# Start and end of a two-layer decoder trunk: load order, an input block shared between engines, and the last squares and a product moved to VectorE and GpSimd

## The chip, the core and the metric

The kernel runs on one core of a Trainium2 chip. The metric is the device time of one execution in microseconds (us); the kernel before takes 969.67 us (median of 3 runs, 969.65 to 970.43). Engines are named as in the profile: PE (TensorE; PEld is its weight load), DVE (VectorE), ACT (ScalarE), POOL (GpSimd), SP (SyncE, which issues most transfers). ACT has a transfer queue of its own, written ACTq beside SPq.

## What is computed

Sixteen learned meta rows are put before 512 rows of x, and two layers follow: gated linear attention, then differential softmax attention. Each begins with an RMS norm and ends in a residual add. A last RMS norm drops the meta rows. Both stretches that the change touches are norms:

```python
def rmsnorm(x, g):
    xf = x.astype(jnp.float32)
    y = xf * lax.rsqrt(jnp.mean(xf * xf, axis=-1, keepdims=True) + EPS)
    return (y * g.astype(jnp.float32)).astype(x.dtype)

h = jnp.concatenate([meta, x], axis=1)      # 16 + 512 rows of 1024
for i in range(DEPTH):
    hn = rmsnorm(h, g_norm[i])
    ...
return rmsnorm(h[:, N_META:], g_final)
```

## The kernel before, in words

Work on the 528 rows is float32; products are split into a high and a low part, so each matrix product is three passes on PE. Weights stream in by SP and are split by ACT (high part) and DVE (low part). PE's order is written out by hand over the whole program; ACT's and DVE's orders are written out by hand at the start (from `squares(0)` on), and DVE's again in the last call `F0(1)`. Elsewhere a scheduler orders them, so a change of the program's text can move rows there too.

**The start.** The rows come in five blocks: block 0 is the 16 meta rows, blocks 1 to 4 are 128 rows of x each, `xt[0]` to `xt[4]` (in the profile: tiles `z`, `qs`, `ks`, `v`, `v`). SP issues, in order: `ident` (identity matrix, 64 KB), meta (64 KB), x blocks 1 and 2 (512 KB each), `grows` (both norms' gains, 8 KB, tile `vm`), x blocks 3 and 4, `glr_raw` (tile `a`, 16 columns of weights in pieces of 64 bytes), then weights `raw`. For each block

- `squares(b)` (L712) lets ACT square the block's 1024 columns and sum them per row,
- `factor(b)` (L564, L565) turns the sum into a row factor: one small op on DVE, then a power on POOL,
- `scaled(b)` (L722) lets DVE multiply the block by its factor, in two halves of 512 columns,
- `raw_turn` (L730) and `turned` (L742) transpose on PE the raw rows and the first half of the scaled rows,
- `raw_copy` (L736, L738) moves the raw transposes to SBUF.

PE transposes only the first half of each block there; the second halves follow for all blocks at once. When block 4's first half is transposed, `scaled_pair` (L800 on ACT, L801 on DVE) multiplies by the gain `g_sb`, and from there the first projections follow. `g_sb` (L775) and `xm`, the meta columns times the gain (L777, tile `t`), are made on DVE after `factor(4)`; `glr` (L779 on ACT, L780 on DVE, tile `kd`) is the split of `glr_raw`. PE runs filler products `warm_up` (L656) between these steps.

**The end.** `final_rows(b, ...)` adds the last products to row block b (`hacc`, tile `keep`, L1857), squares and sums it (L1858 on ACT), makes the row factor (tile `fst`) and multiplies by it and by the gain `gfin`. Block 0 is last and is cut in columns 0 to 512, 512 to 768 and 768 to 1024:

```python
def finish(i, cs):
    hc = hacc[:, b, cs]
    dve.tensor_tensor(hc, hc, ps[i], op=ALU.add)
    act.activation(o[:, cs], hc, AF.Square, scale=..., accum_out=st[:, i:i + 1])
```

After the three sums DVE adds them (L1870, L1871), makes `hg`, the first half times the gain (L1872), POOL takes the power (L1873), ACT scales `hg` (L1882), DVE makes the second half (L1880), and each half goes out by a transfer of its own (L1883; ACT's queue for the first, SP's for the second).

Of the kernel before, what the change touches and what calls it, by code (L numbers as in the profile page):

```python
# [11 lines left out]
F32 = mybir.dt.float32  # L12
# [3 lines left out]
AF = mybir.ActivationFunctionType  # L16
ALU = mybir.AluOpType
# [10 lines left out]
KT = D // P  # L28
# [3 lines left out]
RANK = 16  # L32
EPS = 1e-6
# [184 lines left out]
def trunk(ctx, tc, x, meta, g_norm, gla_w_in, gla_w_gate_up, gla_b_gate, gla_gnorm, gla_w_out,  # L218
# [365 lines left out]
    gp = gctx.enter_context(tc.tile_pool(name="gp", bufs=1))  # L584
# [62 lines left out]
    mhalf = cp.tile([P, 8], F32, name="mhalf")  # L647
# [5 lines left out]
    def warm_up(n, t=None):  # L653
        t = warm if t is None else t
        for _ in range(n):
            pe.matmul(t[:, :P], ones, ones, start=True, stop=True)  # L656
# [2 lines left out]


    ident = cp.tile([P, P], F32, name="ident")
    sp.dma_start(ident, c_ident)
    xt = []
    grows = T(gp, [16, P], F32, "vm0")
    z2 = T(gp, [P, 2, D], F32, "z")
    v2 = [T(gp, [P, 2, D], F32, f"v{i}") for i in range(2)]
    for b in range(5):
        t0, n = BLK[b]
        t = T(gp, [P, D], F32, ("qs", "ks")[b - 1]) if b in (1, 2) else {0: z2, 3: v2[0], 4: v2[1]}[b][:, 1, :]
        sp.dma_start(t[:n], meta if b == 0 else x[(b - 1) * P:b * P])  # L670
        xt.append(t)
        if b == 2:
            sp.dma_start(grows, g_norm.rearrange("l (k p) -> (l k) p", p=P))
    glr_raw = T(gp, [P, KT, RANK], F32, "a0")
    sp.dma_start(glr_raw, g_w_in[:, 6144:6160].rearrange("(k p) c -> p k c", p=P))

# [21 lines left out]
    glr = T(gp, [P, KT, 112], F32R, "kd")  # L698
# [4 lines left out]

    yt = [T(gp, [P, 4, L], F32, f"y{i}") for i in range(2)]
    xm0 = v2[0][:, 0, :]
    sums0 = T(gp, [P, 10], F32, "sums0")
    raws = {}

    def squares(b):
        sq = z2[:, 0, :]  # L710
        n = BLK[b][1]
        act.activation(sq[:n], xt[b][:n], AF.Square, accum_out=sums0[:n, b:b + 1])  # L712

    def factor(b):
        n = BLK[b][1]
        rstd_of(sums0[:n, 5 + b:6 + b], sums0[:n, b:b + 1], D, n)

    def scaled(b, halves=range(2)):
        n = BLK[b][1]
        for i in halves:  # L720
            o = yt[i][:, b - 1, :512] if b else xm0[:NM, i * 512:(i + 1) * 512]
            dve.tensor_scalar(o, xt[b][:n, i * 512:(i + 1) * 512], sums0[:n, 5 + b:6 + b], None, op0=ALU.mult)  # L722

    def raw_turn(b, halves=range(2)):
        n = BLK[b][1]
# [6 lines left out]
    def raw_copy(b, i, eng):  # L732
        t0, n = BLK[b]
        o, pt = hT[:, 4 * i:4 * i + 4, t0:t0 + n], raws[b][i][:, :, :n]
        if eng is act:
            act.activation(o, pt, AF.Copy)  # L736
        else:
            dve.tensor_copy(o, pt)  # L738

    def turned(b, ks):  # L740
        for k in ks:
            pe.transpose(pts[k][:, (b - 1) * P:b * P], yt[k // 4][:, b - 1, k % 4 * P:(k % 4 + 1) * P], ident)  # L742
# [9 lines left out]
    pm0 = ps_tile()  # L752
    pm = pm0[:, :KT * NM].rearrange("p (k m) -> p k m", k=KT)
    for k in range(KT):
        pe.transpose(pm[:, k, :], xm0[:NM, k * P:(k + 1) * P], ident[:NM, :NM])
    raw_copy(1, 0, dve)
    squares(2)
    scaled(1)
# [5 lines left out]
    squares(3)  # L764
    scaled(2)
    factor(3)
    pe.transpose(pm0[:, KT * NM:KT * NM + 16], grows, ident[:16, :16])
    turned(2, range(4))
    warm_up(3)
    scaled(3)  # L770
    turned(3, range(4))
    squares(4)
    factor(4)
    g_sb = cp.tile([P, 2, KT], F32, name="g_sb")
    dve.tensor_copy(g_sb, pm0[:, KT * NM:KT * NM + 16].rearrange("p (l k) -> p l k", l=2))  # L775
    xm = tmp()[:, :KT * NM].rearrange("p (k m) -> p k m", k=KT)
    dve.tensor_tensor(xm, pm, g_sb[:, 0, :].unsqueeze(2).to_broadcast([P, KT, NM]), op=ALU.mult)  # L777
    for c in (0, 32, 64):
        act.activation(glr[:, :, c:c + RANK], glr_raw, AF.Copy)  # L779
    dve.tensor_tensor(glr[:, :, 96:], glr_raw, glr[:, :, :RANK].bitcast(F32), op=ALU.subtract)  # L780
    raw_copy(2, 0, act)
    raw_copy(2, 1, act)
    warm_up(3)
    scaled(4)
    turned(4, range(4))

    b12 = x_parts(6)
# [253 lines left out]
    halves = [(pg, slice(i * HT, (i + 1) * HT)) for i, pg in enumerate(pgs)]  # L1041
# [373 lines left out]
    hacc = T(kp, [P, 4, D], F32, "keep")  # L1415
# [98 lines left out]
    for m in range(2):  # L1514
# [4 lines left out]
        for i in range(2):  # L1519
            cs = slice(i * HT, (i + 1) * HT)  # L1520
# [323 lines left out]
    def final_rows(b, wt, yp):  # L1844

        cut = (0, 512, D) if b else (0, 512, 768, D)
        parts = [slice(c, e) for c, e in zip(cut, cut[1:])]
        ps = [(ps_tile() if i else pb_tile("bx"))[:, :cs.stop - cs.start] for i, cs in enumerate(parts)]
        o = T(xp, [P, D], F32, ("x1", "x3", "x2", "x1")[b], bufs=1)
        st = T(ep, [P, 8], F32, "fst")  # L1850
        hg = T(ep, [P, 512], F32, "t", bufs=3) if b == 0 else None
        if b:
            dve.memset(st[:, 2:3], 0.0)

        def finish(i, cs):
            hc = hacc[:, b, cs]
            dve.tensor_tensor(hc, hc, ps[i], op=ALU.add)  # L1857
            act.activation(o[:, cs], hc, AF.Square, scale=1.0 if b else float(D) ** -0.5, accum_out=st[:, i:i + 1])  # L1858

        def part(hd):  # L1860
            for i, cs in enumerate(parts):
                for n, (p, q, k) in enumerate([(0, q, k) for k in range(2) for q in range(2)] + [(1, 0, 0), (1, 0, 1)]):
                    pe.matmul(ps[i], yp[hd][p][:, k, b * P:(b + 1) * P],  # L1863
                              wt[q][cs.start // 512][:, 2 * hd + k, cs.start % 512:(cs.stop - 1) % 512 + 1],
                              start=hd == n == 0, stop=hd == 1 and n == 5)
                if hd:
                    finish(i, cs)
            if hd:
                if b == 0:
                    dve.scalar_tensor_tensor(st[:, 3:4], st[:, 0:1], EPS, st[:, 1:2], op0=ALU.add, op1=ALU.add)  # L1870
                    dve.tensor_tensor(st[:, 4:5], st[:, 2:3], st[:, 3:4], op=ALU.add)  # L1871
                    dve.tensor_tensor(hg, hacc[:, b, :512], gfin[:, :512], op=ALU.mult)  # L1872
                    pool.tensor_tensor(st[:, 4:5], st[:, 4:5], mhalf[:, :1], op=ALU.pow)  # L1873
                else:
                    dve.tensor_reduce(st[:, 3:4], st[:, 0:3], axis=AX.X, op=ALU.add)
                    rstd_of(st[:, 4:5], st[:, 3:4], D)
                for i in range(2):
                    cs = slice(512 * i, 512 * (i + 1))
                    if b or i:
                        dve.scalar_tensor_tensor(o[:, cs], hacc[:, b, cs], st[:, 4:5], gfin[:, cs], op0=ALU.mult, op1=ALU.mult)  # L1880
                    else:
                        act.activation(o[:, cs], hg, AF.Copy, scale=st[:, 4:5])  # L1882
                    (sp if b or i else act).dma_start(out[0, b * P:(b + 1) * P, cs], o[:, cs])  # L1883

        return part
# [19 lines left out]
    for hd in range(D_HEADS):  # L1905
# [13 lines left out]
        if not last:  # L1919
            n = heads[hd + 1]  # L1920
# [25 lines left out]
        for n, (f, b) in enumerate(steps):  # L1946
# [9 lines left out]
            if last and n == 5:  # L1956
                gfin = T(xp, [P, D], F32, "x0", bufs=1)
# [68 lines left out]
```

## Time and profile before

| what | value |
|---|---|
| median of 3 runs | 969.67 us |
| the profiled execution's own time | 971.08 us |
| its span in the profile | 968.4 us |
| busy share of the span, PE / DVE / ACT / POOL | 98% / 82% / 66% / 8% |
| granted clock of PE over the span | 0.996 |

The profile shows one execution, 2.7 us of which lie around the span, and which took 1.4 us more than the median. PE's busy share includes filler products at the start and pipelined products whose ends are modelled. A row of the timeline gives the start, the duration of the group, the engine, the line and what it writes and reads; the bracket at its end says how long the engine had been idle before and what released it.

### The profile page before, as it was taken

The numbers are of one execution on the slowest core, as the hardware profiler recorded it, in microseconds if no ns is written. First come the engines' busy times: TensorE is split into PE (matmuls) and PEld (weight loads), VectorE is DVE, ScalarE is ACT, GpSimd is POOL, SyncE is SP. The second block draws the span as 40 slices with busy tenths as digits, with TensorE's granted clock in tenths as the row PEclk, the third lists the DMA queues.
The fourth block names the chain that finished last, engine by engine and source line by source line (L and its number), as shares of the span: only waits on it lengthen the run. The fifth ranks groups of instructions, "written<-read, shape, count | busy, mean of one in ns | idle before, by whom it ended". The sixth has DMA issues, their size and how long they took to land.

```text
span 968.4 us, 18488 instructions
## 1 busy us (share of the span) xinstructions
PE 953.0 (98%) x7173; PEld 912.4 (94%) x7173; DVE 798.2 (82%) x1557; ACT 635.6 (66%) x1313; POOL 81.3 (8%) x164
## 2 busy tenths in 40 slices
PE   9999999999999999999999999999999999999997
PEld 8999999999999999998899898999999999989986
DVE  7989886886878787667997887879879889888875
ACT  7776755477647567656757685576766766755673
POOL 1000000000000000000001121111101101110111
PEclk9999999999999999999999999999999999999999
DMA  8322223635462237134356515234252261533312
GB/s 197 88 79 61 86 72 126 142 109 119 123 164 89 87 112 162 47 107 152 99 133 152 127 56 142 83 123 113 87 149 87 80 159 44 145 91 98 110 44 87
DMA packets 128602, 104.96 MB, mean 108 GB/s; under 512 B 51181, under 2 KB 112909, under 8 KB 128512
## 3 DMA queue, kind: packets, MB, share of 16 engines
q1 hardware_dynamic: 123184, 93.80, 35.3%
q10 hardware_dynamic: 5328, 9.95, 2.8%
q8 instruction: 57, 0.93, 0.4%
q14 instruction: 33, 0.27, 0.1%
HBM read 83.64 MB, written 11.80 MB: 99 GB/s over the span
## 4 chain that ended last, share of the span: by engine, by line
PE 73%; DVE 8%; ACT 4%; DMA 3%; issue 2%; POOL 1%; SPq 0%; POOLq 0%; DVEq 0%; ACTq 0%
PE bx L440 17%; PE bv L440 10%; PE by L440 9%; PE ps L409 7%; PE bx L997 5%; PE bx L430 4%; PE bx L409 3%; DMA raw<-in_diff_w_in_dram 3%; PE bv L997 2%; PE by L997 2%; PE ps L1239 2%; PE bv L409 1%; PE by L409 1%; DVE wl L285 1%; PE ps L1863 1%
## 5 line engine op out<-in xcount | busy, mean ns | idle before, releaser
L285 DVE TENSOR_TENSOR wl<-raw,wh 128x1024 fp32r<-128x1024 f32 x93 | 113.5, 1221 | 20.5 <-ACT wh L284 20.0
L284 ACT ACTIVATE wh<-raw 128x1024 fp32r<-128x1024 f32 x93 | 97.9, 1053 | 45.2 <-PE by L997 23.2
L440 PE MATMUL bv<-x,wh 128*128 128x264 f32 (+1 forms) x736 | 108.9, 285 | 0.1
L440 PE MATMUL bx<-x,wh 128*128 128x264 f32 (+1 forms) x720 | 105.6, 285 | 0.4 <-ACT ps L1777 0.4
L440 PEld LDWEIGHTS bv<-x,wh 128*128 128x128 f32 x736 | 96.8, 188 | 0.9 <-DVE z L497 0.3
L440 PEld LDWEIGHTS bx<-x,wh 128*128 128x128 f32 x720 | 94.4, 188 | 1.1 <-ACT ps L1777 0.7
L285 DVE TENSOR_TENSOR wl<-sum,wh 128x1024 fp32r<-128x1024 f32 x46 | 56.2, 1221 | 11.6 <-ACT wh L284 11.2
L461 ACT ACTIVATE u<-bx 128x264 f32<-128x264 f32 (+1 forms) x128 | 48.4, 378 | 21.8 <-PE bx L440 18.9
L440 PE MATMUL bv<-x,wl 128*128 128x264 f32 (+1 forms) x368 | 62.2, 286 | 0.1
L1735 ACT ACTIVATE p<-p,st 128x528 f32<-128x528 f32 (+3 forms) x64 | 36.4, 569 | 38.7 <-DVE st L1733 38.5
L440 PE MATMUL bx<-x,wl 128*128 128x264 f32 (+1 forms) x360 | 59.2, 284 | 0.0
L284 ACT ACTIVATE wh<-sum 128x1024 fp32r<-128x1024 f32 x46 | 48.4, 1051 | 10.4 <-PE bv L440 6.3
L440 PE MATMUL by<-x,a12h 128*128 128x264 f32 (+1 forms) x360 | 52.6, 285 | 0.9 <-DVE t L495 0.9
L440 PE MATMUL bx<-x,a11h 128*128 128x264 f32 (+1 forms) x360 | 53.0, 285 | 0.0
L440 PEld LDWEIGHTS bv<-x,wl 128*128 128x128 f32 x368 | 51.4, 188 | 0.4 <-issue 0.3
L284 ACT ACTIVATE a11h<-raw 128x512 fp32r<-128x512 f32 x46 | 28.9, 627 | 33.3 <-DMA raw<-in_diff_w_in_dram 12.8
L440 PEld LDWEIGHTS bx<-x,wl 128*128 128x128 f32 x360 | 50.0, 188 | 0.6 <-DVE wl L285 0.4
L440 PEld LDWEIGHTS bx<-x,a11h 128*128 128x128 f32 x360 | 47.8, 189 | 0.6
L440 PEld LDWEIGHTS by<-x,a12h 128*128 128x128 f32 x360 | 46.9, 188 | 1.1 <-DVE t L495 1.1
L565 POOL TENSOR_TENSOR st<-st,mhalf 128x1 f32<-128x1 f32 (+1 forms) x20 | 12.1, 606 | 386.5 <-DVE st L564 386.5
L1738 POOL TENSOR_TENSOR st<-st,minus 128x1 f32<-128x1 f32 x32 | 21.1, 658 | 279.4 <-ACT p L1735 226.4
L440 PE MATMUL by<-x,a22h 128*128 128x264 f32 (+1 forms) x280 | 40.1, 284 | 0.0
(501 smaller groups left out, 2671.8 us busy)
## 6 DMA issues: line engine op xcount, KB each, us to landing
raw<-in_diff_w_in_dram SPq DMA_DIRECT2D x52, 512.0 KB, 5.0
raw<-in_gla_w_in_dram SPq DMA_DIRECT2D x48, 512.0 KB, 4.5
raw<-in_gla_w_out_dram SPq DMA_DIRECT2D x8, 1024.0 KB, 6.0
raw<-in_diff_w_out_dram SPq DMA_DIRECT2D x8, 1024.0 KB, 5.3
raw<-in_diff_w_in_dram SPq DMA_DIRECT2D x6, 1024.0 KB, 6.0
vd<-planes ACTq DMA_DIRECT2D x12, 268.0 KB, 4.3
vd<-keep ACTq DMA_DIRECT2D x12, 264.0 KB, 2.3
T<-bdr SPq DMA_DIRECT2D x8, 264.0 KB, 3.8
```

The lines of the kernel that those rows point to most:

```text
L284: act.activation(hi, src, AF.Copy)
L285: dve.tensor_tensor(lo, src, hi.bitcast(F32), op=ALU.subtract)
L409: pe.matmul(ps, l, r, start=first and n == 0, stop=last and n == 2, **kw)
L430: pe.matmul(bank, a[:, k, :], b[k] if n0 is None else b[k][:, n0 + i * nn:n0 + (i + 1) * nn], start=n == 0 and ks[0] == 0, stop=n == len(t ...
L440: pe.matmul(bank[:, :x[q].shape[2]], w[p][:, k * P:(k + 1) * P], x[q][:, k, :], start=first and i == 0, stop=i == len(PASSES) - 1, skip_gr ...
L461: W.moved = act.activation(t, self.bx[:, :self.n], AF.Copy, scale=self.sc)
L565: pool.tensor_tensor(dst, dst, mhalf[:np_, :dst.shape[1]], op=ALU.pow)
L997: pe.matmul(banks[i][:, :HT], h.t[p][:, k, mm * P:(mm + 1) * P], s.y[q][k][:, i * HT:(i + 1) * HT], start=n == 0, stop=n == len(PASSES) - 1)
L1239: pe.matmul(o, s.kd[:, i, kc], s.qs[:, i, t0:t0 + n], start=i == 0, stop=i == 1)
L1735: act.activation(p[:, :nk], p[:, :nk], AF.Exp, scale=-1.0, bias=st[:, m:m + 1], accum_out=st[:, 2 + m:3 + m])
L1738: pool.tensor_tensor(st[:, 5:6], st[:, 3:4], minus, op=ALU.pow)
L1863: pe.matmul(ps[i], yp[hd][p][:, k, b * P:(b + 1) * P], wt[q][cs.start // 512][:, 2 * hd + k, cs.start % 512:(cs.stop - 1) % 512 + 1], star ...
```

## The change

Four things, in the diff's order.

1. SP issues x blocks 1 to 4 first; `ident`, meta and `grows` are issued by ACT, ahead of its table load. 
2. `squares(4)` is divided: ACT takes columns 0 to 512, DVE columns 512 to 1024 with a multiply-and-sum. `scaled(4)`'s first half goes to ACT, and one of block 2's raw copies goes from ACT to DVE.
3. `grows` is transposed before block 1 is, and `g_sb` and `xm` are made ahead of block 3's scaling. The low part of `glr` moves behind the first `scaled_pair`, and one filler product in PE's order goes.
4. In block 0 of the last norm the squares of the last 256 columns go to DVE, which adds the earlier sums on the way; `hg` goes to POOL and starts as soon as the first 512 columns are summed; the second half is made and sent in two pieces of 256 columns, so that SP issues two transfers.

```diff
-    sp.dma_start(ident, c_ident)
...
-    for b in range(5):
...
-        sp.dma_start(t[:n], meta if b == 0 else x[(b - 1) * P:b * P])
...
+    act.dma_start(ident, c_ident)
+    act.dma_start(xt[0][:NM], meta)
+    act.dma_start(grows, g_norm.rearrange("l (k p) -> (l k) p", p=P))
+    for b in range(1, 5):
+        sp.dma_start(xt[b], x[(b - 1) * P:b * P])
...
+    def squares(b, e=D):
...
+        act.activation(sq[:n, :e], xt[b][:n, :e], AF.Square, accum_out=sums0[:n, b:b + 1])
+        if e < D:
+            dve.tensor_tensor_reduce(sq[:n, e:], xt[b][:n, e:], xt[b][:n, e:], op0=ALU.mult, op1=ALU.add, scale=1.0,
+                                     scalar=D * EPS, accum_out=sums0[:n, 10:11])
...
+            dve.tensor_scalar(o, sums0[:n, b:b + 1], sums0[:n, 10:11], 1.0 / D, op0=ALU.add, op1=ALU.mult)
+            pool.tensor_tensor(o, o, mhalf[:n, :1], op=ALU.pow)
...
+    warm_up(2)
+    squares(4, 512)
+    scaled(3, [0])
+    factor(4, 512)
+    scaled(3, [1])
+    turned(3, range(4))
+    raw_copy(2, 0, act)
...
+    scaled(4, [0], act)
+    scaled(4, [1])
+    raw_copy(2, 1, dve)
     turned(4, range(4))
...
+            if i < 2:
+                act.activation(o[:, cs], hc, AF.Square, scale=1.0 if b else float(D) ** -0.5, accum_out=st[:, i:i + 1])
+            else:
+                dve.scalar_tensor_tensor(st[:, 3:4], st[:, 0:1], EPS, st[:, 1:2], op0=ALU.add, op1=ALU.add)
+                dve.tensor_tensor_reduce(o[:, cs], hc, hc, op0=ALU.mult, op1=ALU.add, scale=1.0 / D, scalar=st[:, 3:4],
+                                         accum_out=st[:, 4:5])
+            if b == i == 0:
+                pool.tensor_tensor(hg, hc, gfin[:, cs], op=ALU.mult)
```

On DVE, from block 2's factor on, the kernel before has this order (`v_12` and `v_13` hold x blocks 3 and 4, `y_21` and `y_22` the scaled halves, `sums_23` sums and factors):

```order
L564 TENSOR_SCALAR sums_23_163<-sums_23_163 128x1
L722 TENSOR_SCALAR y_21_161<-v_12_121,sums_23_163 128x512
L722 TENSOR_SCALAR y_22_162<-v_12_121,sums_23_163 128x512
L564 TENSOR_SCALAR sums_23_163<-sums_23_163 128x1
L775 COPY g_sb<-ps_184 128x16
L777 TENSOR_TENSOR t_242<-ps_184,g_sb 128x128
L780 TENSOR_TENSOR kd_157<-a_16_131,kd_157 128x8x16
L722 TENSOR_SCALAR y_21_161<-v_13_122,sums_23_163 128x512
```

The changed kernel has this order there (x blocks 3 and 4 are now `v_11` and `v_12`; ISA is the multiply-and-sum and the read of its sum):

```order
L564 TENSOR_SCALAR sums_23_163<-sums_23_163 128x1
L779 COPY g_sb<-ps_184 128x16
L781 TENSOR_TENSOR t_230<-ps_184,g_sb 128x128
L711 ISA z_118,sums_23_163<-v_12_120 128x512
L711 ISA sums_23_163 128x1
L731 TENSOR_SCALAR y_21_161<-v_11_119,sums_23_163 128x512
L720 TENSOR_SCALAR sums_23_163<-sums_23_163 128x1
L731 TENSOR_SCALAR y_22_162<-v_11_119,sums_23_163 128x512
L731 TENSOR_SCALAR y_22_162<-v_12_120,sums_23_163 128x512
L747 COPY hT_90<-ps_214 128x4x128
```

Between block 3's factor (the first row of each piece) and block 3's first scaling there are now four more rows, one of which needs block 4.

The scheduler also moves three small DVE rows some 15 us later, around the first decay product (`bx` holds its two halves, `a_20` takes them). This is the piece of the difference, without the renumbered lines around it:

```order
+L1107 TENSOR_SCALAR gn_sb<-gn_sb 128x16
+L1141 TENSOR_SCALAR dgs<-dg_sb 128x2
+L1133 TENSOR_TENSOR lt_4702<-lv 128x2
+L1057 CAST a_20_159<-bx_316 16x264 x2
+L1057 CAST a_20_159<-bx_317 16x264 x2
+L1062 TENSOR_TENSOR a_20_159<-bx_316,a_56_424 16x264
+L1062 TENSOR_TENSOR a_20_159<-bx_317,a_56_424 16x264
```

Before, the rows on `gn_sb` and `dg_sb` stood between the last two of these, and the one on `lv` behind them; now all three stand ahead of the first cast. All other rows of the five engines, up to the tail, keep their order.

## Rows read from the trace of the kernel before

**Rows 1.** The page: busy time and share of each engine.

```profile
PE 953.0 (98%) x7173; PEld 912.4 (94%) x7173; DVE 798.2 (82%) x1557; ACT 635.6 (66%) x1313; POOL 81.3 (8%) x164
```

**Rows 2.** Timeline of the start: issues and squares (start us, us, engine, line, op).

```profile
0.87 0.39 SPq L662 DMA_DIRECT2D ident<-in_ident_dram  x1
1.32 0.41 SPq L670 DMA_DIRECT2D z<-in_meta_dram  x1
1.77 0.42 SPq L670 DMA_DIRECT2D qs<-in_x_dram  x1
...
3.42 1.06 ACT L712 ACTIVATE z<-z 16x1024 f32<-16x1024 f32 x1 [1.31 <-DMA z<-in_meta_dram]
...
5.61 1.06 ACT L712 ACTIVATE z<-qs 128x1024 f32<-128x1024 f32 x1 [1.04 <-DMA qs<-in_x_dram]
...
11.06 1.06 ACT L712 ACTIVATE z<-v 128x1024 f32<-128x1024 f32 x1 [0.42 <-DMA v<-in_x_dram]
```

**Rows 3.** Timeline of the start: factors and scaling on POOL, DVE, then PE.

```profile
4.82 0.54 POOL L565 TENSOR_TENSOR sums<-sums,mhalf 16x1 f32<-16x1 f32 x1 [4.37 <-DVE sums L564]
5.40 0.87 DVE L722 TENSOR_SCALAR v<-z,sums 16x512 f32<-16x512 f32 x2 [0.66 <-POOL sums L565]
...
12.29 0.15 DVE L564 TENSOR_SCALAR sums<-sums 128x1 f32<-128x1 f32 x1
...
12.76 0.28 DVE L780 TENSOR_TENSOR kd<-a,kd 128x128 fp32r<-128x128 f32 x1
...
13.64 0.44 PE L742 MATMUL bx<-ident,y 128*128 128x128 f32 x2
...
16.16 1.36 DVE L285 TENSOR_TENSOR x<-y,x 128x528 fp32r<-128x528 f32 x2 [0.42 <-ACT x L284]
```

**Rows 4.** Windows: busy us of each engine, granted clock, DMA share, GB/s.

```profile
8.20:11.60 3.40, 3.40 (x16) 2.87 (x17) 1.57 (x6) 2.41 (x6) 1.10 (x2) 0.51 1.15 300
```

**Rows 5.** Transfers by line, three stretches: count, KB each, median us from issue to landing.

```profile
vd<-keep ACTq DMA_DIRECT2D x6, 264.0 KB, 2.2
...
raw<-in_gla_w_in_dram SPq DMA_DIRECT2D x2, 512.0 KB
yd<-t ACTq DMA_DIRECT2D x2, 256.0 KB, 5.6
...
out_dram<-x ACTq DMA_DIRECT2D x1, 256.0 KB, 2.6
```

**Rows 6.** Groups by line and form: busy us, mean ns of one, idle before.

```profile
L1733 DVE CUSTOM_DVE_ANT_0 p<-ps,T,st 128x264 f32<-128x264 f32 x16 | 7.7, 487 | 0.5
...
L799 POOL COPY y<-t 128x64 f32<-128x64 f32 x2 | 0.5, 238 | 2.8 <-PE ps L742 1.5 <-PE by L742 1.3
```

**Rows 7.** Timeline around 30 us, DVE, then PE.

```profile
28.15 1.79 DVE L1046 CAST a<-bx 16x264 fp32r<-16x264 f32 x4 [1.37 <-ACT a L1043]
...
30.43 0.17 DVE L1096 TENSOR_SCALAR gn_sb<-gn_sb 128x16 f32<-128x16 f32 x1
...
30.71 0.43 DVE L1051 TENSOR_TENSOR a<-bx,a 16x264 fp32r<-16x264 f32 x1
...
31.19 0.99 PE L903 MATMUL bx<-x,wh 128*128 128x264 f32 x6 [0.35 <-DVE a L1051]
```

**Rows 8.** Timeline of the tail: DVE, POOL, ACT's queue.

```profile
960.76 0.42 DVE L1857 TENSOR_TENSOR keep<-keep,ps 128x256 f32<-128x256 f32 x1
...
961.94 0.16 DVE L1870 SCALAR_TENSOR_TENSOR fst<-fst 128x1 f32<-128x1 f32 x1
...
962.55 0.69 DVE L1872 TENSOR_TENSOR t<-keep,x 128x512 f32<-128x512 f32 x1
962.77 0.87 POOL L1873 TENSOR_TENSOR fst<-fst,mhalf 128x1 f32<-128x1 f32 x1 [4.51 <-DVE fst L1871]
963.68 0.75 DVE L1880 SCALAR_TENSOR_TENSOR x<-keep,fst,x 128x512 f32<-128x512 f32 x1 [0.44 <-POOL fst L1873]
...
964.43 0.36 ACTq L1883 DMA_DIRECT2D out_dram<-x  x1
```

More of the change, by code (lines that the diff above doesn't have):

```diff
@@ L661, in trunk @@
     ident = cp.tile([P, P], F32, name="ident")
-    sp.dma_start(ident, c_ident)
-    xt = []
-    grows = T(gp, [16, P], F32, "vm0")
     z2 = T(gp, [P, 2, D], F32, "z")
     v2 = [T(gp, [P, 2, D], F32, f"v{i}") for i in range(2)]
-    for b in range(5):
-        t0, n = BLK[b]
-        t = T(gp, [P, D], F32, ("qs", "ks")[b - 1]) if b in (1, 2) else {0: z2, 3: v2[0], 4: v2[1]}[b][:, 1, :]
-        sp.dma_start(t[:n], meta if b == 0 else x[(b - 1) * P:b * P])
-        xt.append(t)
-        if b == 2:
-            sp.dma_start(grows, g_norm.rearrange("l (k p) -> (l k) p", p=P))
+    grows = T(gp, [16, P], F32, "vm0")
+    xt = [z2[:, 1, :], T(gp, [P, D], F32, "qs"), T(gp, [P, D], F32, "ks"), v2[0][:, 1, :], v2[1][:, 1, :]]
+    act.dma_start(ident, c_ident)
[3 more added lines that the diff above has]
+        sp.dma_start(xt[b], x[(b - 1) * P:b * P])
     glr_raw = T(gp, [P, KT, RANK], F32, "a0")
@@ L705, in trunk, with factor, scaled @@
     xm0 = v2[0][:, 0, :]
-    sums0 = T(gp, [P, 10], F32, "sums0")
+    sums0 = T(gp, [P, 11], F32, "sums0")
     raws = {}
-    def squares(b):
+    def squares(b, e=D):
         sq = z2[:, 0, :]
         n = BLK[b][1]
-        act.activation(sq[:n], xt[b][:n], AF.Square, accum_out=sums0[:n, b:b + 1])
-    def factor(b):
-        n = BLK[b][1]
-        rstd_of(sums0[:n, 5 + b:6 + b], sums0[:n, b:b + 1], D, n)
-    def scaled(b, halves=range(2)):
+        act.activation(sq[:n, :e], xt[b][:n, :e], AF.Square, accum_out=sums0[:n, b:b + 1])
+        if e < D:
+            dve.tensor_tensor_reduce(sq[:n, e:], xt[b][:n, e:], xt[b][:n, e:], op0=ALU.mult, op1=ALU.add, scale=1.0,
+                                     scalar=D * EPS, accum_out=sums0[:n, 10:11])
+    def factor(b, e=D):
+        n = BLK[b][1]
+        o = sums0[:n, 5 + b:6 + b]
+        if e == D:
+            rstd_of(o, sums0[:n, b:b + 1], D, n)
+        else:
+            dve.tensor_scalar(o, sums0[:n, b:b + 1], sums0[:n, 10:11], 1.0 / D, op0=ALU.add, op1=ALU.mult)
+            pool.tensor_tensor(o, o, mhalf[:n, :1], op=ALU.pow)
+    def scaled(b, halves=range(2), eng=None):
         n = BLK[b][1]
@@ L721, in scaled @@
             o = yt[i][:, b - 1, :512] if b else xm0[:NM, i * 512:(i + 1) * 512]
-            dve.tensor_scalar(o, xt[b][:n, i * 512:(i + 1) * 512], sums0[:n, 5 + b:6 + b], None, op0=ALU.mult)
+            src, f = xt[b][:n, i * 512:(i + 1) * 512], sums0[:n, 5 + b:6 + b]
+            if eng is act:
+                act.activation(o, src, AF.Copy, scale=f)
+            else:
+                dve.tensor_scalar(o, src, f, None, op0=ALU.mult)
     def raw_turn(b, halves=range(2)):
@@ L755, in trunk @@
         pe.transpose(pm[:, k, :], xm0[:NM, k * P:(k + 1) * P], ident[:NM, :NM])
+    pe.transpose(pm0[:, KT * NM:KT * NM + 16], grows, ident[:16, :16])
     raw_copy(1, 0, dve)
@@ L766, in trunk @@
     factor(3)
-    pe.transpose(pm0[:, KT * NM:KT * NM + 16], grows, ident[:16, :16])
     turned(2, range(4))
[L769 to L773, printed above, removed]
     g_sb = cp.tile([P, 2, KT], F32, name="g_sb")
@@ L777, in trunk @@
     dve.tensor_tensor(xm, pm, g_sb[:, 0, :].unsqueeze(2).to_broadcast([P, KT, NM]), op=ALU.mult)
+    warm_up(2)
[5 more added lines that the diff above has]
+    raw_copy(2, 0, act)
     for c in (0, 32, 64):
         act.activation(glr[:, :, c:c + RANK], glr_raw, AF.Copy)
-    dve.tensor_tensor(glr[:, :, 96:], glr_raw, glr[:, :, :RANK].bitcast(F32), op=ALU.subtract)
-    raw_copy(2, 0, act)
-    raw_copy(2, 1, act)
     warm_up(3)
-    scaled(4)
+    scaled(4, [0], act)
+    scaled(4, [1])
+    raw_copy(2, 1, dve)
     turned(4, range(4))
@@ L803, in trunk @@
     scaled_pair(0)
+    dve.tensor_tensor(glr[:, :, 96:], glr_raw, glr[:, :, :RANK].bitcast(F32), op=ALU.subtract)
     for k0 in range(0, KT, 2):
@@ L1857, in finish @@
             dve.tensor_tensor(hc, hc, ps[i], op=ALU.add)
-            act.activation(o[:, cs], hc, AF.Square, scale=1.0 if b else float(D) ** -0.5, accum_out=st[:, i:i + 1])
+            if i < 2:
+                act.activation(o[:, cs], hc, AF.Square, scale=1.0 if b else float(D) ** -0.5, accum_out=st[:, i:i + 1])
+            else:
+                dve.scalar_tensor_tensor(st[:, 3:4], st[:, 0:1], EPS, st[:, 1:2], op0=ALU.add, op1=ALU.add)
[3 more added lines that the diff above has]
+                pool.tensor_tensor(hg, hc, gfin[:, cs], op=ALU.mult)
         def part(hd):
@@ L1869, in part @@
                 if b == 0:
-                    dve.scalar_tensor_tensor(st[:, 3:4], st[:, 0:1], EPS, st[:, 1:2], op0=ALU.add, op1=ALU.add)
-                    dve.tensor_tensor(st[:, 4:5], st[:, 2:3], st[:, 3:4], op=ALU.add)
-                    dve.tensor_tensor(hg, hacc[:, b, :512], gfin[:, :512], op=ALU.mult)
                     pool.tensor_tensor(st[:, 4:5], st[:, 4:5], mhalf[:, :1], op=ALU.pow)
@@ L1876, in part @@
                     rstd_of(st[:, 4:5], st[:, 3:4], D)
-                for i in range(2):
-                    cs = slice(512 * i, 512 * (i + 1))
+                for i, cs in enumerate(parts):
                     if b or i:
```

## The prediction

> **What bounds the kernel now.** I read the page first: PE is busy for 98% of the span [rows 1]. So the edits can pay only where PE waits for something, or runs filler: in the first 15 us, before the projections, and after PE's last product. The two ends are read from the timeline. At the start ACT waits for a transfer before each block's squares: 1.31 us for meta, 1.04 for x block 1, 0.42 for x block 4, whose squares begin at 11.06 [rows 2]. Behind block 4 stands a fixed chain, squares, factor, power on POOL, scaling on DVE, and PE's transposes begin at 13.64 [rows 3]. From there ACT, DVE and PE hand work to each other with no wait on a load, so I take it that 1 us gained or lost at 13.64 arrives whole at the end. At the tail PE is done before DVE's last sum, and the chain is sums, power, scaling, transfer [rows 8].
>
> **The loads.** x block 1 is issued 0.90 us earlier (0.87 for 1.77 [rows 2]), and with it the later blocks. Before, block 1's squares began 3.84 us after its issue and block 4's 5.45 us after block 1's. With these spacings kept, the blocks land from about 4.7 to 10.2; blocks 3 and 4 gain a little more since nothing small stands between them. Meta is now issued by ACT, second behind `ident`, so at about 1.3 as before (ACT's issues take as long as SP's, 0.4 us [rows 2, 8]). Before, it landed 2.1 us after its issue. Now it shares the DMA engines with x. The same queue gives both bounds [rows 5]: `vd`, 264 KB in a stretch with little other traffic, lands in 2.2 us; at the tail 256 KB take 2.6, beside SP's transfer of the other half, which leaves when DVE is done at 964.43, the same moment [rows 8]; `yd` takes 5.6 in a stretch in which SP loads two times 512 KB, so 3.4 more. Meta thus lands between 3.4 and 6.8. The tail's pair is nearest in its start, `yd` in its partner, an x block of 512 KB ahead of it and one behind: I take 0.8 us of delay, closer to the first because meta and `ident` are small, and so a landing at 4.2.
>
> The Trainium skill, "DMA: Bandwidth & Descriptors", section "Issuing engines are not separate DMA queues", says that transfers of all issuing engines run on the same DMA engines and interleave, and that a second issuer saves only issue time. By it the x blocks gain their 0.9 us of issue time and meta pays for company; the tail's 2.6 for 2.2 agrees.
>
> **The chain behind meta.** This is where the change puts its new wait. DVE takes the blocks strictly in turn, so a late meta delays all of them. From M, the start of meta's squares: power at M+1.40, scaling at M+1.98 [rows 2, 3], DVE free 0.80 later (the pair takes 0.87, and the next op starts under its end). Each further block costs a round of 0.82 (factor 0.15, power 0.54 [rows 3], hand-overs) and 0.80: block 1's factor at M+2.8, block 2's at M+4.4, block 3's at M+6.0. Then comes what the order shows: gain copy and `xm`, 0.47 from factor to next op (12.29 to 12.76 [rows 3]); the half-block squares, 0.69, as DVE's other product of 512 columns [rows 8]; block 3's first scaling, 0.40; block 4's factor and power, 0.82; ACT's scaling of 512 columns, 0.63 (1.06 for 1024 [rows 2], and some of that fixed), and 0.05 to PE. Sum: PE starts block 4's transposes at M+9.1. With M = 4.2 that is 13.3 for 13.64: **0.3 us gained**. With M = 3.4 it would be 12.5, but then two others bind: PE's own order, at the lower of its two clock levels, 1.2 GHz, from 8.2 to 11.6 (granted 0.51 [rows 4]), where eight raw transposes, eight scaled ones and two sets of filler run slower, which no row prices (I let it bind near 13.0, midway); and x block 3. So an early meta gives 0.6 to 1.0.
>
> Costed at nothing: block 4's half squares on ACT (0.63 for 1.06; the DVE chain ends later); the raw copy moved to DVE (about 0.7, beside PE's transposes of block 4; without that cover it would land on L801's first op); the low part of `glr` (0.28, between the two L801; DVE waits 0.42 for ACT before its first split at 16.16 [rows 3], which covers it); `grows` transposed early (one PE op, and if its load were late PE would stand with block 1's transposes behind it; it is issued only 0.4 us after meta); two filler pairs fewer or more.
>
> **Around 30 us.** PE waits 0.35 us for DVE's second `a` [rows 7], which stands behind two small ops (30.43 to 30.71). These now run in DVE's idle 1.37 us ahead of the casts. The wait shrinks by 0.28 at most; ACT and DVE are nearly full from there to 40 us and will take some back: **0.2** (bounds 0 and 0.3).
>
> **The tail.** The sum of the first two parts stays at 961.94 [rows 8]. The new squares of 256 columns with a running sum cost 0.49 [rows 6], start at about 962.14 and with the read of the sum end at 962.62; before, the last sum ended at 962.63. So the power starts where it did, 962.77. But it took 0.87 beside DVE's `hg` product (962.55 to 963.24) [rows 8] against 0.54 undisturbed [rows 3]; `hg` is off DVE now, so 0.33 is gained. Then DVE's first piece of 256 columns takes 0.42 instead of 0.75, so its transfer leaves 0.33 earlier still, and the last piece ends about as early as ACT's half. The transfers share one set of engines, so not all of that counts: **0.55** for the tail (bounds 0.2 and 0.75). `hg` on POOL starts at about 960.9, when the first sum is written. No row shows such a product on POOL: below, it cannot be shorter than the 64-column copy, 0.24 us; above, eight such copies for each of two operands, 3.8 [rows 6]. Nearest is the same product on DVE, 0.69 [rows 8]; POOL's small ops are slower than DVE's, so I take twice that, 1.4, and the cover is the 1.87 us until the power starts.
>
> The Trainium skill, "GPSIMD Engine Reference", section "Engine selection", gives the rule against this edit: a two-input product is about twice as slow on GpSimd and belongs on VectorE. By it `hg` costs 0.7 more, inside its cover. "SBUF — State Buffer" adds, in its single rule, that the two engines' shared port is an exclusive lock. The power of 0.87 beside `hg` agrees. By it DVE's small sum at 961.94 could wait for `hg` until about 962.3, which would take 0.35 off the tail's 0.55.
>
> **Sum.** 0.3 + 0.2 + 0.55 = 1.05 us. Against the profiled execution's own 971.08 that is 970.0; that execution took 1.4 us more than the median, and taken from the median of 969.67 the change gives **968.6**.
>
> **Rivals.**
> - *Meta slips through early* (by 3.8): ident's and meta's packets go out before x has started to flow. For it: the tail's pair, in which ACT's transfer lost only 0.4 us [rows 5]. Against it: `yd`. Start 0.6 to 1.0, total 1.3 to 2.0: 967.7 to 968.4, about 968.1.
> - *Meta lands late*, slower than before: its queue stands behind x blocks 1 and 2 as `yd` stood behind its loads. Each us of M beyond 4.5 costs a whole us through the chain M+9.1. Mid and tail give 0.75, so from a landing at 5.3 on the kernel is slower; halfway from there to 6.8, at 6.0, PE starts at 15.1, and the time is 970.4; at 6.8, 971.2. For it: `yd` [rows 5]. Against it: the tail's pair, which flows together.
> - *`hg` on POOL is the bound*: at the upper end of 3.8 it ends at 964.7, the power waits, and the tail loses 1.3 instead of gaining: 970.4. It decides from 1.87 us on.
> - *The loads do not move*: the DMA share is 1.15 from 8.2 to 11.6 [rows 4], and if the engines are as full before that, x lands no earlier for being issued earlier, and meta takes what is gained. Start 0, with mid and tail 0.75: 968.9; with both at half, 969.3.
> - *PE stays at its lower clock beyond 11.6*: gaps move as the blocks move. Some two dozen products between 11.6 and 14 at half the level cost about 1 us: near 969.7.
>
> **How the numbers follow.** Forecast (meta at 3.9 to 4.6, 968.2 to 969.0): 0.42. Early meta: 0.30. Late meta: 0.11. POOL bound: 0.04. Loads not moved: 0.09. Clock: 0.04. A measurement of this kernel tells about 0.2% from no change, 1.9 us, so faster means below 967.7 and slower above 971.6. Faster needs the early meta with every bound at its good end: 0.13. Slower needs the late meta at its far end or two mishaps: 0.04. Same: 0.83. The range 967.5 to 970.0 leaves out about 0.07 below and 0.10 above.
>
> **What would show it.** In the profile after: x block 1's squares near 4.9, block 4's before 10.5; meta's squares at 4.2 (3.5 for the early rival, beyond 5.2 for the late one); block 4's transposes on PE at 13.3; no wait for `a` on PE near 30 us; a power of 0.55 in the tail and `hg` on POOL between 1.0 and 1.8 us. The prediction is wrong if PE's block 4 transposes start before 12.6 or after 14.2, or if a shift at 13.64 does not arrive at the end of the span.

## The result, and the profile after

The changed kernel takes 972.15 us (median of 14 executions, 970.58 to 973.77); the kernel before took 969.88 beside it (14 executions). The ratio is 1.0021, 95% interval 1.0013 to 1.0029, so it is slower by 2.0 us (1.3 to 2.8). The ratio is not the quotient of the two medians; where the two differ, both are given below. A second measurement gave 1.0025 (1.0014 to 1.0036). The forecast was 968.6, the range 967.5 to 970.0.

The profiled execution (970.58 us, span 968.7) was the fastest of the 14, so its trace shows the kinds of change, not their full size. Its timeline at the start, ACT's queue, ACT, DVE, POOL and PE:

```profile
1.27 0.45 ACTq L667 DMA_DIRECT2D z<-in_meta_dram  x1
...
5.34 1.06 ACT L709 ACTIVATE z<-z 16x1024 f32<-16x1024 f32 x1 [1.84 <-DMA z<-in_meta_dram]
...
6.52 1.06 ACT L709 ACTIVATE z<-qs 128x1024 f32<-128x1024 f32 x1
...
10.41 0.63 ACT L709 ACTIVATE z<-v 128x512 f32<-128x512 f32 x1
...
11.81 0.68 DVE L711 CUSTOM_DVE_ANT_0 z<-v 128x512 f32<-128x512 f32 x1
...
13.10 0.72 POOL L721 TENSOR_TENSOR sums<-sums,mhalf 128x1 f32<-128x1 f32 x1 [0.98 <-DVE sums L720]
...
13.86 0.72 ACT L729 ACTIVATE y<-v,sums 128x512 f32<-128x512 f32 x1 [1.65 <-POOL sums L721]
...
14.66 0.41 PE L751 MATMUL bx<-ident,y 128*128 128x128 f32 x2
```

Meta is issued at the old time (1.27 for 1.32), and its squares start at 5.34 for 3.42 [rows 2]. No block of x is waited for any more: block 1's squares follow meta's with no bracket. Block 4's are earlier (10.41 for 11.06), as the change wanted, and it does not help: the DVE chain behind meta reaches block 4 late, and PE's block 4 transposes start at 14.66 for 13.64 [rows 3], 1.0 us later.

The 13.64 is itself late. It comes from an execution 1.4 us above its median, with PE at the lower clock level from 8.2 to 11.6 [rows 4]. The kernel tail_only, which is described below and has the same start, was profiled with PE at 1.00 there, and PE starts these transposes at 13.31:

```profile
13.31 0.44 PE L742 MATMUL bx<-ident,y 128*128 128x128 f32 x2 [0.29 <-DVE y L722]
```

Against that the changed kernel loses 1.35 us in this trace and 1.59 in its second one (14.90).

The timeline of the tail, same kernel:

```profile
961.65 0.42 DVE L1868 TENSOR_TENSOR keep<-keep,ps 128x256 f32<-128x256 f32 x1
...
961.71 1.28 POOL L1876 TENSOR_TENSOR t<-keep,x 128x512 f32<-128x512 f32 x1 [2.57 <-DVE keep L1868]
...
962.83 0.18 DVE L1872 SCALAR_TENSOR_TENSOR fst<-fst 128x1 f32<-128x1 f32 x1
963.04 0.48 DVE L1873 CUSTOM_DVE_ANT_0 x<-keep,fst 128x256 f32<-128x256 f32 x1
...
963.68 0.55 POOL L1888 TENSOR_TENSOR fst<-fst,mhalf 128x1 f32<-128x1 f32 x1 [0.69 <-DVE fst L1873]
```

The second sum (961.65) comes 0.89 us later than before (960.76 [rows 8]) and the span ends only 0.3 later, so the tail takes about 0.6 less. The power takes 0.55 for 0.87.

Around 30 us PE's wait for `a` [rows 7] is gone, and 0.3 of the 1.0 us is gained: the next group of `bx` products starts 0.69 later than before. But the gain is lost again within 4 us. PE's rows of the kernel before, then of the change (the second `bx` group, the second product with `a`, the next `bv`):

```profile
34.79 2.18 PE L903 MATMUL bx<-x,wh 128*128 128x264 f32 x16
...
37.07 0.73 PE L1069 MATMUL ps<-a,z 128*128 128x264 f32 x2
...
38.36 0.28 PE L903 MATMUL bv<-x,wh 128*128 128x264 f32 x1
```
```profile
35.48 2.18 PE L914 MATMUL bx<-x,wh 128*128 128x264 f32 x16
...
38.05 0.73 PE L1080 MATMUL ps<-a,z 128*128 128x264 f32 x2
...
39.34 0.29 PE L914 MATMUL bv<-x,wh 128*128 128x264 f32 x1
```

The delays are 0.69, 0.98 and 0.98: the product with `a` waits for DVE, which delivers at its old pace, and the 1.0 us from the start is whole again.

PE's clock is the last difference. Windows of the changed kernel (busy us of PE, PEld, DVE, ACT, POOL, then granted clock, DMA share, GB/s):

```profile
4.80:8.20 3.40, 3.01 (x17) 2.61 (x16) 1.02 (x5) 2.80 (x5) 0.54 (x1) 1.00 0.99 377
8.20:11.60 3.40, 2.66 (x22) 2.20 (x21) 2.63 (x9) 3.37 (x9) 1.15 (x3) 0.87 1.19 254
11.60:15.00 3.40, 3.40 (x20) 3.20 (x19) 2.90 (x8) 1.33 (x5) 1.24 (x2) 0.63 1.19 297
```

PE is at 2.4 GHz but for 3.4 us at 1.2 (0.26 of the second window, 0.74 of the third, by the shares 0.87 and 0.63), which lie around 10.7 to 14.1 and not from 8.2 to 11.6 as before [rows 4]. Ahead of the fall PE had stood idle for DVE twice, 0.39 us up to 7.85 and 0.74 up to 9.47. Gaps alone do not decide it: in the profile of loads_only (below) PE is busy for only 1.57 of the 3.40 us from 4.8 to 8.2, and the clock is 1.00 in every window up to 960 us.

Over whole executions the mean granted clock was 0.997 or less in 12 of the 14 of the changed kernel, and 0.998 or 0.999 in 51 of the 64 of the kernel before that ran beside the first eight experiments. The mean also counts the time behind PE's last product: loads_only's profile has 1.00 up to 963 us, 0.50 from 964 on, and a mean of 0.998. So a mean does not say where the lower level lay.

### The profile page after: what moved, and what is told of

It reads as the page before. It is cut to its first block, busy times and chain, and to the rows that moved or that the text cites. A ratio compares the mean times of both kernels' runs of the same rounds, so it can differ in the third digit from the quotient of the medians.

```text
span 968.7 us, 18487 instructions
## 1 busy us (share of the span) xinstructions
PE 954.5 (99%) x7171; PEld 913.5 (94%) x7171; DVE 799.2 (83%) x1560; ACT 635.1 (66%) x1311; POOL 82.8 (9%) x165
## 4 chain that ended last, share of the span: by engine, by line
PE 75%; DVE 8%; ACT 3%; DMA 2%; issue 2%; POOL 1%; SPq 0%; POOLq 0%; DVEq 0%; ACTq 0%
PE bx L440 18%; PE bv L440 11%; PE by L440 10%; PE ps L409 8%; PE bx L1008 5%; PE bx L430 4%; PE bx L409 3%; PE bv L1008 2%; PE by L1008 2%; DMA raw<-in_diff_w_in_dram 2%; PE ps L1250 2%; PE bv L409 1%; PE by L409 1%; DVE wl L285 1%; PE bx L1881 1%
```

## The experiments

Theories: **A**, meta lands late on ACT's queue. **B**, the rows put ahead of block 3's scaling on DVE cost the time. **C**, the tail loses in typical executions. **D**, the rest arises later in the program. **E**, the lower clock level that follows PE's gaps.

**The change in parts.** Each takes some hunks of the diff shown and leaves the others as before.

| kernel | load order | block 4 shared, rows moved | tail | us (969.48 before) | ratio to before (95%) |
|---|---|---|---|---|---|
| tail_only | old | no | new | 968.80 | 0.9987 (0.9978 to 0.9997) |
| loads_only | new | no | old | 972.22 | 1.0028 (1.0019 to 1.0038) |
| share_only | old | yes | old | 970.17 | 1.0006 (0.9997 to 1.0015) |
| loads_back | old | yes | new | 969.67 | 1.0006 (0.9997 to 1.0016) |

> The kernel before with the tail's part alone (last squares on VectorE, hg on GpSimd, the second half in two pieces). Theory A (the time is lost at the start, because meta lands late on ACT's queue, and the tail pays as forecast): 0.5 us faster than before, 969.3 to 969.5, with 7.7 to 7.8 us from the last block-0 sum of columns 0 to 512 to the end of the span, for 8.3 before. Theory C (the tail loses in most executions what it gains in the profiled one): 0.5 to 2 us slower than before.

> The kernel before with the new load order alone. Theory A (late meta): meta's squares start at 5.0 to 5.6 for 3.42, the VectorE chain behind them is late, PE's block 4 transposes start at 14.0 to 15.0 and the time is 0.5 to 2.5 us above before. Theory B (the rows put ahead of block 3's scaling on VectorE are what costs, not the loads): within 0.3 us of before, or up to 0.5 faster, since x lands earlier.

> The kernel before with the block 4 part alone: divided squares and scaling, g_sb and xm ahead of block 3's scaling, the old load order. Theory A (late meta): PE's block 4 transposes start at 13.0 to 13.6 for 13.64, and the time is 0 to 0.6 us below before. Theory B (the reordered VectorE chain): transposes at 14.2 or later, and 0.7 to 2 us above before.

> The changed kernel with the old load order (SP issues ident, meta, x 1 and 2, gains, x 3 and 4). Theory A (late meta): the loss goes and the tail's gain stays: 0.5 to 1.1 us below before, 968.8 to 969.4, so 2.5 to 3.5 below the changed kernel. Theory B (reordered chain): it stays as slow as the changed kernel, 971 to 972.5. Theory C (tail): likewise above before, with share_only at before's time.

Alone, the loads lose 2.7 us, the tail gains 1.3 by the ratio (0.3 to 2.1; 0.7 by the medians), and the sharing gains nothing, where A expected it to be up to 0.6 faster. C is out. B is not what makes the changed kernel slower than before, but its part does cost: loads_back should have kept the tail's gain and lies 1.8 us above tail_only (1.0006 for 0.9987).

**The load order in variants.** All keep the rest of the change. after_again is the changed kernel once more.

```diff
 meta_sp                             meta_first
-act.dma_start(xt[0][:NM], meta)    +act.dma_start(xt[0][:NM], meta)
 act.dma_start(grows, ...)           act.dma_start(ident, c_ident)
+sp.dma_start(xt[0][:NM], meta)     -act.dma_start(xt[0][:NM], meta)
 grows_act
-act.dma_start(ident, c_ident)
-act.dma_start(xt[0][:NM], meta)
+sp.dma_start(ident, c_ident)
+sp.dma_start(xt[0][:NM], meta)
```

> The changed kernel once more, for a second profile. Its first profiled execution (970.58 us) was the fastest of 14 with a median of 972.15. Theory A (late meta): in a typical execution meta's squares start later than 5.34 and PE's block 4 transposes later than 14.63, by about 1.5 us. Theory D (the rest is lost later, not at the start): the start looks as in the first profile, and the span is longer by 1 to 2 us in a stretch that the stretches of the two profiles side by side will name.

> The changed kernel with meta issued by SP ahead of the x blocks; ident and the gains stay on ACT's queue. Theory A (late meta): meta's squares start at 2.9 to 3.4, x block 1's at about 5.2, block 4's transposes on PE near 12.7 to 13.4, and the time is 2.5 to 3.5 us below the changed kernel (968.6 to 969.7). If ident's late landing on ACT's queue counts as much as meta's: 970.5 to 971.5. Theory B: as the changed kernel.

> The changed kernel with meta ahead of ident on ACT's queue, so that meta is issued 0.4 us earlier and behind nothing on its queue. Theory A, with the wait made by x's packets on the same transfer engines: meta's squares start at 4.4 to 5.0 and the time is 0.3 to 1.0 us below the changed kernel, with ident later instead. If meta is late because of its place behind ident alone: squares at 3.4 to 3.8, time 1.5 to 2.5 below.

> The changed kernel with ident and meta issued first by SP; only the gains stay on ACT's queue. Theory A (late meta): meta's squares at 3.4 as before, x block 1's at 5.6, block 4's transposes at 13.0 to 13.4, time 968.8 to 969.6. Theory B (reordered chain): transposes 14.2 or later and the time above 971.

after_again: 971.42, ratio 1.0025. meta_sp: 969.38, 1.0002 (0.9993 to 1.0011). meta_first: 969.55, 1.0006 (0.9997 to 1.0015). grows_act: 969.74, 1.0003 (0.9995 to 1.0012). Each of three ways to take meta from behind `ident` on ACT's queue brings back 1.5 to 2.2 us, so A stands; none gets the forecast's 1 us. meta_first is the sharpest: two transfers change places, nothing else. Its meta's squares start at 4.03, between the two branches that were expected, with `ident` late instead. That is 3.2 us after the issue, for 4.1 in second place (5.34 for 1.27) and 2.1 on SP's queue ahead of x [rows 2], so place on the queue and x beside it both count. ACT's queue as such is not slow: `vd`, 264 KB with little beside it, lands in 2.2 [rows 5]. In after_again's trace meta's squares start at 5.62, again in an execution below its median, so the traces could not tell A from D for the rest of the loss.

**The start by itself.** The kernels are cut after the first normed input, so that the time of each execution, and not of the profiled one alone, is the start's.

```diff
     ws.held = 0
+    ordered.close()
+    act.dma_start(out[0, :P, :NR], xg[1][:, 3, NM:])
+    return
```

> The kernel before, cut off after the first normed input and its splits (near 25 us of the full kernel); both layers and the last norm are left out, and one 256 KB piece of that input is written out. It gives the start's time in every execution, not in the profiled one alone. It is the base for the two runs that follow: spans within about 0.5 us of each other, some executions later by what a lower-clock stretch costs at the start (0.3 to 1.5 us).

> The changed kernel, cut off at the same place; both layers and the last norm are left out. Theory A (late meta, and in typical executions later than in the profiled ones): the median is 2.0 to 3.0 us above that of the cut kernel before, the profiled execution only 1.0 to 1.5 above. Theory D (the start costs 1.0 to 1.5 in every execution, and the rest arises later): median 1.0 to 1.5 above, with little spread.

> The changed kernel with meta ahead of ident on ACT's queue, cut off at the same place; both layers and the last norm are left out. Theory A: the median is about 1.9 us below that of the cut changed kernel, as in the full kernels, though the profiled execution of the full one had PE waiting for ident until 6.74; so ident must land earlier in typical executions. If that profile was typical: within 0.3 us of the cut changed kernel.

Measured: 27.71 us (27.64 to 27.93), 30.25 (29.75 to 30.82) and 28.41 (28.34 to 29.79). The start loses 2.54 in the middle and at least 1.8 in every execution: A, not D. Transfers of the three cut kernels (KB each, us from issue to landing):

```profile
z<-in_meta_dram SPq DMA_DIRECT2D x1, 64.0 KB, 2.1
```
```profile
z<-in_meta_dram ACTq DMA_DIRECT2D x1, 64.0 KB, 4.7
```
```profile
ident<-in_ident_dram ACTq DMA_DIRECT2D x1, 64.0 KB, 5.4
```

Whichever is second on ACT's queue, behind the other and beside x, lands 2.6 to 3.3 us later than meta did on SP's queue ahead of x. With meta first it is `ident`, for which PE waits; that profiled execution took 29.79 and another 29.64, the other five 28.3 to 28.5, so the lateness is not the same each time. In the cut changed kernel meta's squares start at 5.92 and PE's block 4 transposes at 15.20; in the cut kernel before at 3.30 and 13.22.

**The clock.** Five filler products more, where PE stood idle:

```diff
     raw_turn(1)
+    warm_up(3)
...
     pe.transpose(pm0[:, KT * NM:KT * NM + 16], grows, ident[:16, :16])
+    warm_up(2)
```

> The changed kernel with five more filler products on PE: three behind block 1's raw transposes and two behind meta's, where PE stands idle for DVE. Theory E (beside the late meta, a stretch at the lower clock level in most executions, 13 of 14 of the changed kernel show a mean clock of 0.997 or less, costs 0.5 to 1.3 us; it follows PE's gaps): the mean clock rises to 0.998 or 0.999 and the time falls by 0.5 to 1.3 us, to 970.5 to 971.5. If the clock doesn't matter or doesn't follow the gaps: 971.4 to 972.4.

> The changed kernel with five more filler products, cut off as start_before is; both layers and the last norm are left out. If the late meta alone makes the start's loss: as the cut changed kernel, 30.0 to 30.5. If the lower clock makes 1.2 us of it or more, as the full kernels say: 28.7 to 29.3. Middle: 29.4 to 29.9.

It was 12 of 14, not 13. The full kernel: 970.27 us, 1.0003 (0.9994 to 1.0011), so 1.7 to 2.1 us below the changed one by the ratios, with a mean clock of 0.998 or more in 9 of 12 executions. Its windows, for the first two above:

```profile
4.80:8.20 3.40, 3.40 (x22) 3.28 (x21) 0.96 (x4) 2.73 (x5) 0.54 (x1) 1.00 1.00 383
8.20:11.60 3.40, 3.21 (x29) 2.76 (x29) 2.66 (x10) 3.37 (x9) 1.11 (x2) 1.00 1.23 255
```

PE is busy from 4.8 to 8.2 and stays at 2.4 GHz. Meta's squares start at 5.40 there, so the filler does not move the transfers. It does not move the chain behind meta either. Block 4's transposes, then the tail's second sum, with filler:

```profile
14.69 0.44 PE L751 MATMUL bx<-ident,y 128*128 128x128 f32 x2 [0.35 <-ACT y L729]
...
960.88 0.42 DVE L1870 TENSOR_TENSOR keep<-keep,ps 128x256 f32<-128x256 f32 x1
```

The transposes start 9.29 behind meta's squares, for 9.32 with 3.4 us at the lower level, so up to there the level cost the traced execution nothing. The second sum comes 0.77 earlier (for 961.65), and that difference arises between 40 and 960 us, where neither trace has a stretch at the lower level.

What such a stretch can cost where PE has no slack, another trace shows: tail_grows_act (below), whose window from 922 to 926 us stands here behind that of tail_only.

```profile
922.00:926.00 4.00, 2.87 (x21) 2.65 (x22) 3.49 (x9) 2.15 (x6) 0.55 (x1) 1.00 0.46 156
```
```profile
922.00:926.00 4.00, 3.10 (x15) 2.88 (x16) 3.27 (x9) 1.44 (x5) 0.55 (x1) 0.72 0.62 173
```

In both PE had just stood idle for DVE, 1.11 us, and only one fell. Its five `bv` products there take 1.27 us for 0.76; its rows stand 0.2 us ahead of tail_only's at 921 us and 1.26 behind them at the second sum (960.87 for 959.61): 1.5 us for one stretch of 3.4. Neither trace of the changed kernel has one so far back.

The cut kernel with filler took 29.80 (29.69 to 30.22), 0.45 below the cut changed kernel: a miss for "1.2 us or more". Three of the changed kernel's six cut executions took 30.54 to 30.82 at mean clocks of 0.772 and 0.773, above all with filler; the other three took 29.75 to 29.95. So it is shown that the filler raises the mean clock and saves time. That the clock is what saves it, and where, is not shown: the changed kernel's two executions at 0.998 had spans of 970.1 and 970.9, those with filler at 0.998 or 0.999 had 967.4 to 968.8. E stays open.

**Sharing and loads, cut.** share_only and loads_only, cut at the same place, and a kernel with the old squares and scaling, meta first on SP's queue, x behind it, `ident` and the gains on ACT's queue.

> The kernel before with the block 4 part alone, cut off at the same place; both layers and the last norm are left out. If the sharing gains nothing because VectorE's detour (half of block 3's scaling ahead of block 4's factor, a power of 0.72 beside VectorE) eats what the divided squares give: 27.6 to 28.0, as the cut kernel before. If it gains what the order promised: 27.0 to 27.4. If it costs what the full kernel's median says: 28.2 to 28.6.

> The kernel before with the new load order alone, cut off at the same place; both layers and the last norm are left out. If the loads make the whole loss of the start: 29.9 to 30.5. If the sharing takes part in it: 29.0 to 29.7.

> The kernel before (old squares and scaling) with meta first on SP's queue, x blocks 1 to 4 behind it, ident and the gains on ACT's queue, cut off at the same place; both layers and the last norm are left out. If x landing 0.4 us earlier counts and ident is in time: 27.0 to 27.5 for 27.7. If ident on ACT's queue lands late behind x as meta did: 28.0 or more.

Measured: 28.34 (28.25 to 28.61), 29.79 (29.38 to 31.07), 27.02 (26.75 to 27.20), for 27.71 before. These three and the filled one ran on another chip than the first three, and the full kernel before took 969.29 beside them for 969.76, so a few tenths between the two sets can be the chip's. The sharing costs 0.6 by itself, as in the full kernel (1.0006). Timeline from block 4's squares on, cut kernel before, then the shared one:

```profile
10.61 1.06 ACT L712 ACTIVATE z<-v 128x1024 f32<-128x1024 f32 x1 [0.39 <-DMA v<-in_x_dram]
...
12.09 0.55 POOL L565 TENSOR_TENSOR sums<-sums,mhalf 128x1 f32<-128x1 f32 x1 [1.06 <-DVE g_sb L775]
...
13.22 0.44 PE L742 MATMUL bx<-ident,y 128*128 128x128 f32 x2 [0.28 <-DVE y L722]
```
```profile
10.90 0.63 ACT L712 ACTIVATE z<-v 128x512 f32<-128x512 f32 x1 [0.41 <-DMA v<-in_x_dram]
11.00 0.68 DVE L714 CUSTOM_DVE_ANT_0 z<-v 128x512 f32<-128x512 f32 x1
...
11.60 0.48 DVE L734 TENSOR_SCALAR y<-v,sums 128x512 f32<-128x512 f32 x1
12.00 0.21 DVE L723 TENSOR_SCALAR sums<-sums 128x1 f32<-128x1 f32 x1
...
12.29 0.72 POOL L724 TENSOR_TENSOR sums<-sums,mhalf 128x1 f32<-128x1 f32 x1 [0.99 <-DVE sums L723]
...
13.04 0.72 ACT L732 ACTIVATE y<-v,sums 128x512 f32<-128x512 f32 x1 [0.34 <-POOL sums L724]
...
13.82 0.44 PE L754 MATMUL bx<-ident,y 128*128 128x128 f32 x2 [0.35 <-ACT y L732]
```

From the squares to PE it takes 2.61 before and 2.92 shared. The half on ACT saves 0.43, but half of block 3's scaling (0.40 from 11.60 to 12.00) stands ahead of the factor, the power takes 0.72 beside DVE's scaling for 0.55, and ACT scales in 0.72 what DVE scaled in 0.44. The other 0.29 of that pair is x landing later, which the sharing does not touch. In the full kernels the chain from squares to PE shows the same step (2.60 in tail_only, 2.91 in loads_back).

**A better version.** The tail of the change and the load order of start_x_early, no sharing; beside it the same with `ident` on SP's queue too.

```diff
 tail_meta_sp                        tail_grows_act
 act.dma_start(ident, c_ident)       sp.dma_start(ident, c_ident)
 sp.dma_start(xt[0][:NM], meta)      sp.dma_start(xt[0][:NM], meta)
 act.dma_start(grows, ...)           act.dma_start(grows, ...)
```

> The kernel before with the changed tail, and with meta first on SP's queue, x blocks 1 to 4 behind it, ident and the gains on ACT's queue; no sharing of block 4. If the start's 0.7 us and the tail's 0.7 add up: 967.8 to 968.4 (1.0 to 1.6 below before). If what the start gains is given back later: as the tail alone, 0.7 below before.

> The kernel before with the changed tail, and with the gains alone moved to ACT's queue (SP issues ident, meta, x blocks 1 to 4); no sharing of block 4. Only the gains' issue leaves SP's row, so blocks 3 and 4 are issued 0.45 us earlier and blocks 1 and 2 as before: 0.7 to 1.1 us below before, above the kernel with meta first on SP by 0.2 to 0.5.

tail_meta_sp takes 967.97 us (966.80 to 969.75) for 969.75: 0.9979 (0.9970 to 0.9987), 2.0 us faster than the kernel before by the ratio (1.8 by the medians), and faster than the changed one. tail_grows_act: 968.76, 0.9987 (0.9979 to 0.9996). From meta_sp, with the same loads and tail, tail_meta_sp differs by the sharing, 1.0002 for 0.9979, so beside the new tail the sharing costs 1.8 to 2.2 us and not 0.6. In the traces loads_back stands 0.37 behind tail_only at the block 4 transposes (13.68 for 13.31) and 1.13 at the tail's second sum (960.74 for 959.61); why the rest arises in between stays open. The gains of start and tail add up, and `ident` alone ahead of x on ACT's queue is in time.

## Why the prediction was wrong

- **The step that failed** is the landing of meta at 4.2, "0.8 us of delay, closer to the first because meta and `ident` are small". Its squares started at 5.34, 5.62 and, cut, 5.92, so the delay was 1.9 to 2.6. Small size did not help; of the two bounding rows it was `yd` (3.4 us more beside two loads of 512 KB) that came nearer. I chose between them by likeness of size. What the runs showed in its place is that a transfer beside x pays for x (1.1 us more in first place on ACT's queue, in meta_first's trace) and again for standing behind `ident` (another 0.9). The rival "meta lands late" came true; it had a chance of 0.11.
- **The base was late too.** "0.3 us gained" is 13.3 against 13.64, a row of an execution 1.4 us above the median, taken from the median all the same. Against tail_only's 13.31 or the cut kernel's 13.22 a landing at 4.2 would have gained nothing.
- **The chain M+9.1** held: 9.32 in the changed kernel, 9.28 when cut. What it misses is the power of 0.72 for 0.55. That a shift at 13.64 arrives held for the start's 1 us up to 40 us. But whole traces can't show it to the end: tail_only's second sum of the tail stands 1.15 us earlier than before, of which its start explains 0.34.
- **The rival's price was too low.** It gave 970.4 for a landing at 6.0; the median is 972.15 with a landing below that in every trace. It counted 0.2 gained around 30 us, which was 0: the wait went, and the work behind it waited for DVE, as the bound of 0 said. It counted nothing for the sharing. And it may have left out the clock: I priced that as a rival of its own, at 0.04, while low means came with the late meta (0.997 or less in 28 of the 32 executions of the changed kernel and loads_only, in 13 of 64 of the kernel before). What the clock took is not shown.
- **The tail** held: about 0.6 for 0.55 in the trace; `hg` on POOL 1.28 for 1.4. The Trainium skill, "SBUF — State Buffer", section "Who interferes with whom", in its single rule on the shared port, would have had DVE's small sum wait for `hg`; here it started at 962.83 with `hg` running from 961.71 to 962.99 and took 0.18 for 0.16 before, so no wait shows. The power of 0.72 beside DVE's scaling, against 0.55 in the new tail, agrees with it.
- **Costed at nothing**, the sharing costs 0.6 (28.34 for 27.71). I saw the four rows ahead of block 3's scaling and put them into the chain behind a late meta; with meta on time they and the slower power and scaling make block 4's own chain 0.31 longer.
- **The loads** as argued: the Trainium skill, "DMA: Bandwidth & Descriptors", section "Issuing engines are not separate DMA queues", says that a second issuer saves issue time alone. The runs agree: where meta and x were issued 0.45 to 0.9 us earlier, with meta still first and only `ident` and the gains moved, the start won 0.7; where meta was to share the engines with x, it paid for the company.

Sum, by the ratios of the parts alone: loads 2.7, sharing 0.6, tail −1.3, which is the 2.0 measured (1.3 to 2.8). That they add up so well is in part luck. Beside the new tail the sharing costs 1.8 to 2.2, and with the other two in place the loads cost 1.5 to 1.9 (1.0021 or 1.0025 for 1.0006). Cut, the start loses 2.5: the sharing about 0.5 (30.25 to 29.79), what the filler gives back 0.45, and meta's landing the rest, about 1.5. What the sharing costs behind the start, and where the filler gains 1.7 to 2.1 in the full kernel, stays open.

## What to carry to other kernels

A small transfer on which a serial chain hangs goes out ahead of the large ones; to issue it at the same time from another engine is not the same, since it lands with the company it keeps. Before a row serves as the base, see at which clock its execution ran. When a wait moves on an engine that feeds PE, ask also what PE's new gaps do to its clock. And when effects are of one microsecond in a thousand, cut the kernel behind the stage in question: the cut kernel showed the 0.6 us of the sharing with no overlap of executions (28.25 to 28.61, for 27.64 to 27.93), where the full one's profile was of an execution 1.6 us below the median.

## What the runs showed of the hardware that was not expected

On ACT's queue the second of two transfers of 64 KB landed 4.7 (meta) or 5.4 us (`ident`) after its issue, beside x on SP's queue; ahead of x on SP's queue meta took 2.1. Five filler products on an idle PE, which compute nothing, made the kernel 1.7 to 2.1 us faster, with the granted clock at 1.00 in all windows up to 15 us where one had shown 0.63, though in the traces the chain up to 15 us was no shorter for it. And one stretch of 3.4 us at 1.2 GHz cost 1.5 us around 925 us, and nothing that shows in the changed kernel's chain up to block 4's transposes.
